# Six of eight output tiles of the mixer's first projection half as seven block products for eight

## The chip, the cores and the metric

The kernel runs on one core of one Trainium2 chip. The metric is device time in microseconds (us) of one execution. Engines are called as in the profile: PE (TensorE, the matmuls; PEld is its weight loading), DVE (VectorE), ACT (ScalarE), POOL (GpSimd) and SP (SyncE, which here only issues DMAs).

## The reference, cut to what matters

One layer of a hybrid decoder for 512 prompt tokens and 64 sample tokens, 576 in all, in float32:

```python
y_ssd = rms(y_ssd * silu(z)) * g_ssm_out                       # Mamba heads, 1024 wide
h_ml  = rms(h_ml) * g_mlstm_out * sigmoid(og)                  # mLSTM heads, 1024 wide
mix   = concatenate([y_ssd, h_ml], axis=-1) @ w_out            # 2048 -> 1024
x     = x + rms(mix) * g_post_mix
# then cross attention with w_xq, w_xo, and the gated FFN with w_gate, w_up, w_down
```

The change concerns `y_ssd @ w_out[:1024]`, the first half of the output projection.

## The kernel before, in words

Activations lie with features on the 128 partitions and the 576 tokens along the free axis, in 8 slices of 128 features. Every float32 operand of a matmul is split into a high part (a cast, by ACT) and a low part (source minus high, by DVE or, for half of some weight tiles, by a copy with scale -1 and an accumulating DMA that POOL issues). A product is then three matmuls: high by high, high weights by low activations, low weights by high activations. One output tile of 128 features over 8 slices is 24 matmuls for 256 tokens and 24 for 320 (`HALVES`).

The stretch around the change, in the order of the code:

- **The og tiles.** Eight tiles of the input projection (`in_tile(29 + j, og_evac(j))`), each in two token halves, gate the mLSTM output. A half's result lies in a PSUM bank of a pool of three (`GP`). DVE evicts it into a tile `tmp` (L1133; two buffers), ACT takes tanh, and DVE multiplies into `qk` (L1136). In the second half, POOL copies the 64 sample columns of `tmp` to `ogs` (L1138), and this `tmp` is free only then.
- **The mLSTM scan** of four heads runs beside it (L960 to L1005), as does the scan of the samples (L1029 to L1075). A head does four chunks one after another: matmuls `ps_n` (L983, L985) and `ps_c` (L988), a copy of `ps_n` by DVE (L986) and a state update `cst_` by DVE (L993, or L991 by ACT for the first). Then the head norm: squares by ACT (L938), short DVE steps (L941 to L954) around a power by POOL (L950), a scaling by DVE (L1000), eight transposes by PE (`ps_ht`, L1004). Each updated sample state leaves by a DMA of its tile (`o_cs`, L1059).
- **`mixs`**, the normed Mamba output `y`, is scaled (L1122) and split (L202, L203) in two groups of four slices, `gn_apply(0)` and `gn_apply(1)`.
- **`out1(j)`**, j from 0 to 7: the first half of the output projection, each with its weight tile split by ACT and DVE (L191, L198), the result copied to `f_mix` by ACT (L1154).
- **`out2(j)`**: the second half, from the mLSTM output `mixm`, added to `f_mix` by DVE (L1288). In the `out1` stretch the next stages are prepared: parts of later weights are split and stored (`presplit`), and the memory inputs are loaded (`memraw`).

No table sets the order here: the framework decides, when the program is built, the order of the instructions on each engine, by the times that it expects. On the chip each engine then goes through its list in that order. Where a pool's memory lay under another tile before, the first writer waits for what last used it.

The names that the prediction uses: "tile 2" and "tile 3" are the og tiles with j = 2 and j = 3, "head 3" is the last head of the scan.

Of the kernel before, what the change touches and what calls it, by code (L numbers as in the profile page):

```python
# [24 lines left out]
KT = 8  # L25
# [90 lines left out]
def build(nc, tc, ctx, I, O):  # L116
# [84 lines left out]
    def split(hi, lo, src, eng=None, cast=None):  # L201
        c = (cast or A.copy)(hi, src)  # L202
        (eng or V).tensor_tensor(lo, src, hi.bitcast(F32), op=ALU.subtract)  # L203
        return c
# [912 lines left out]
    def gn_apply(g):  # L1117
# [3 lines left out]
        for j in range(4 * g, 4 * g + 4):  # L1121
            V.scalar_tensor_tensor(y[:, j, :], y[:, j, :], PAR("g_ssm", j), rb, op0=ALU.mult, op1=ALU.mult)  # L1122
# [19 lines left out]
    for j in range(8):  # L1142
        in_tile(29 + j, og_evac(j))
        if j in GN:
            GN[j]()

    f = SL(5, "f_mix")
    evs = []

    def out1(j):  # L1150
# [6 lines left out]
    for j in range(8):  # L1157
        hm = qk[:, 4 * (j % 2) + j // 2, 0:TP]
        with tc.issue_after((evs[0] if j > 2 else htc).ins):
            A.activation(mixm_h[:, j, 0:TP], hm, AF.Copy, scale=ghalf[:, j:j + 1])  # L1160
        V.scalar_tensor_tensor(mixm_l[:, j, 0:TP], hm, ghalf[:, j:j + 1], mixm_h[:, j, 0:TP].bitcast(F32),
                               op0=ALU.mult, op1=ALU.subtract)
    o4 = ogs.rearrange("p (h d) t -> p h d t", d=2)
    for d in range(2):
        V.scalar_tensor_tensor(o4[:, :, d], o4[:, :, d], 1.0, qk[:, 4 * d:4 * d + 4, TP:T], op0=ALU.add, op1=ALU.mult)
    V.tensor_tensor(ogs, ogs, ghalf.unsqueeze(2).to_broadcast([P, KT, TS]), op=ALU.mult)
    split(mixm_h[:, :, TP:T], mixm_l[:, :, TP:T], ogs)
    stv.close()
# [61 lines left out]
    at = st.enter_context(tc.tile_pool(name="attn", bufs=1, reuse_waits="tile"))  # L1230


    PRE = [("xo", 0), ("xo", 1), ("g", 0), ("u", 0), ("g", 1), ("u", 1), ("g", 2), ("u", 2)]
    pre = dr.tile([P, len(PRE), 1024], F32, name="pre")

    ahead = []

    def presplit(n, left=1):

        while len(ahead) > left:  # L1240
            n_, t_ = ahead.pop(0)
            h_ = at.tile([P, 1024], F32R, name="preh", tag="prh", bufs=1)
            with tc.issue_after(evs[-1].ins):
                A.copy(h_, t_)
            V.tensor_tensor(t_, t_, h_.bitcast(F32), op=ALU.subtract)
            G.dma_start(pre[:, n_, :], t_)
        for _ in range(n):
            n_ = turns.pop(0)
            k, j = PRE[n_]
            t_ = at.tile([P, 1024], F32, name="prel", tag=("pr", "prl", "mv")[n_ % 3], bufs=1)  # L1250
            G.dma_start(t_, I[{"xo": "wxo", "g": "wgate", "u": "wup"}[k]][j])
            ahead.append((n_, t_))

    turns = list(range(len(PRE)))
# [7 lines left out]
    for j in range(8):  # L1262
        if j:
            out1(j)
        presplit(min(len(turns), 1 if j else 2))

        if j > 3:
            k2 = slice(2 * j - 8, 2 * j - 6)
            with tc.issue_after(loads[-1].ins):
                S.dma_start(memraw[:, k2, :], I["memT"][:, k2, :])  # L1270

    def memory(ks):
        for k in ks:
# [588 lines left out]
    class Seven:  # L1862
# [73 lines left out]
        def bank(s):  # L1936
            return (MP if s.side else GP)("ps_" + s.name)[:, :288]
# [539 lines left out]
```

## Time and profile before

| | us |
|---|---|
| median of three runs | 1074.99 (1074.83 to 1075.98) |
| the profiled execution, its time | 1074.69 |
| the profiled execution, its span | 1072.9 |
| from the first og eviction to the start of `out1` | 317.2 to 384.3 |
| `out1` | 384.3 to 434.2 |
| `out2` and what lies beside it | 434.2 to 488 |

The span is from the first to the last instruction; the execution's time is 1.8 us more. Durations of single matmuls in the profile overlap, since they are pipelined: what a stream of them costs is read from the distance of their starts. The lines themselves are shown in the prediction.

### The profile page before, as it was taken

Reading aid. Unit: us, or ns where it says so; the run is one execution under the profiler, and the core shown is the slowest. Engines: PE = TensorE matmul, PEld = TensorE weight load, DVE = VectorE, ACT = ScalarE, POOL = GpSimd, SP = SyncE. Lnnn points to the kernel's source line nnn. Section 1 sums busy time; section 2 is a strip of 40 time slices with the busy share of each in tenths; the row PEclk is TensorE's granted clock in tenths of the full one; section 3 lists DMA queues with packets and bytes.
Section 4 is the critical chain, followed back from the end, with each engine's and each line's share of the span. In section 5 each row is a group of like instructions: output and inputs, shape, how many; then the busy total and the mean of one; then the engine's idle time right before and its main releaser. Section 6 shows DMA issues by size and latency. Waiting matters only on the chain.

```text
span 1072.9 us, 20686 instructions
## 1 busy us (share of the span) xinstructions
PE 1063.1 (99%) x8096; PEld 1011.0 (94%) x8096; DVE 757.7 (71%) x1523; ACT 608.9 (57%) x1102; POOL 231.0 (22%) x305
## 2 busy tenths in 40 slices
PE   9999999999999999999999999999999999999997
PEld 8999887778999999999999989999999999999997
DVE  6798775658878774758755556766467887787556
ACT  7778523345654555655555445645566566656654
POOL 0454543313213111000154201100011111111000
PEclk9999999999999999999999999999999999999999
DMA  6776544425655349642468775743476687578532
GB/s 209 176 162 132 158 134 172 147 89 168 196 150 152 106 143 330 235 170 98 158 213 288 265 256 176 254 124 98 133 179 137 160 188 178 114 191 188 144 119 89
DMA packets 58965, 181.74 MB, mean 169 GB/s; under 512 B 6604, under 2 KB 12108, under 8 KB 58356
## 3 DMA queue, kind: packets, MB, share of 16 engines
q1 hardware_dynamic: 42884, 138.22, 38.7%
q0 software_dynamic: 15408, 41.43, 19.7%
q8 instruction: 63, 1.03, 0.4%
q10 hardware_dynamic: 576, 0.79, 0.2%
q14 instruction: 34, 0.28, 0.1%
HBM read 159.75 MB, written 20.65 MB: 168 GB/s over the span
## 4 chain that ended last, share of the span: by engine, by line
PE 98%; DVE 0%; DMA 0%; POOL 0%; issue 0%; ACT 0%; SPq 0%; DVEq 0%
PE ps_in L215 7%; PE ps_in L218 7%; PE ps_in L216 7%; PE ps_v L882 5%; PE ps_g L1946 3%; PE ps_u L1946 3%; PE ps_g L1945 3%; PE ps_o L218 3%; PE ps_o L216 3%; PE ps_u L1947 3%; PE ps_g L1947 3%; PE ps_o L215 3%; PE ps_u L1945 3%; PE ps_dn L1945 2%; PE ps_dn L1947 2%; PE ps_dn L1946 2%
## 5 line engine op out<-in xcount | busy, mean ns | idle before, releaser
L215 PE MATMUL ps_in<-uh,whi 128*128 128x320 f32 (+1 forms) x544 | 162.6, 299 | 0.0
L218 PE MATMUL ps_in<-uh,wlo 128*128 128x320 f32 (+1 forms) x544 | 161.6, 298 | 0.0
L216 PE MATMUL ps_in<-ul,whi 128*128 128x320 f32 (+1 forms) x544 | 161.1, 296 | 0.0
L191 ACT CAST whi<-raw 128x1024 fp32r<-128x1024 f32 (+1 forms) x104 | 105.4, 1015 | 93.3 <-PE ps_in L216 21.5
L198 DVE TENSOR_TENSOR wlo<-raw,whi 128x1024 fp32r<-128x1024 f32 (+2 forms) x97 | 95.3, 983 | 63.7 <-ACT whi L191 63.0
L215 PEld LDWEIGHTS ps_in<-uh,whi 128*128 128x128 f32 x544 | 102.3, 188 | 1.9 <-issue 0.8
L218 PEld LDWEIGHTS ps_in<-uh,wlo 128*128 128x128 f32 x544 | 102.2, 188 | 1.9 <-issue 1.3
L216 PEld LDWEIGHTS ps_in<-ul,whi 128*128 128x128 f32 x544 | 102.4, 188 | 0.5
L196 POOL DMA_DIRECT2D wlo<-win x31 | 27.2, 877 | 80.2 <-ACT wlo L195 69.9
L1945 PE MATMUL ps_g<-b,whi 128*128 128x288 f32 x144 | 42.4, 295 | 0.0
L1946 PE MATMUL ps_g<-b,whi 128*128 128x288 f32 x144 | 42.3, 294 | 0.0
L1946 PE MATMUL ps_u<-b,whi 128*128 128x288 f32 x144 | 42.2, 294 | 0.0
L1945 PE MATMUL ps_u<-b,whi 128*128 128x288 f32 x144 | 42.2, 294 | 0.0
L1905 DVE TENSOR_TENSOR wlo<-sw,whi 128x1024 fp32r<-128x1024 f32 (+1 forms) x26 | 29.6, 1139 | 16.8 <-ACT whi L1904 16.8
L1918 ACT CAST whi<-rawx 128x1024 fp32r<-128x1024 f32 (+1 forms) x26 | 25.6, 986 | 26.2 <-PE ps_dn L1946 13.3
L1895 ACT CAST whi<-raw 128x1024 fp32r<-128x1024 f32 (+1 forms) x26 | 25.6, 985 | 22.8 <-PE ps_g L1946 11.8
L215 PE MATMUL ps_xo<-qh,whi 128*128 128x288 f32 x128 | 38.2, 301 | 0.0
L216 PE MATMUL ps_xo<-ql,whi 128*128 128x288 f32 x128 | 37.8, 297 | 0.0
L218 PE MATMUL ps_o<-mixm_h,wlo 128*128 128x256 f32 (+1 forms) x128 | 37.5, 293 | 0.0
L216 PE MATMUL ps_o<-mixm_l,whi 128*128 128x256 f32 (+1 forms) x128 | 37.5, 293 | 0.0
L218 PE MATMUL ps_xq<-u2h,wlo 128*128 128x320 f32 (+1 forms) x128 | 37.5, 294 | 0.0
L218 PE MATMUL ps_o<-mixs_h,wlo 128*128 128x320 f32 (+1 forms) x128 | 37.4, 293 | 0.0
(788 smaller groups left out, 3855.6 us busy)
## 6 DMA issues: line engine op xcount, KB each, us to landing
raw<-win SPq DMA_DIRECT2D x35, 512.0 KB, 4.4
raw<-wout SPq DMA_DIRECT2D x17, 512.0 KB, 4.2
raw<-wxq SPq DMA_DIRECT2D x13, 512.0 KB, 4.7
raw<-wgate SPq DMA_DIRECT2D x13, 512.0 KB, 3.3
raw<-wup SPq DMA_DIRECT2D x13, 512.0 KB, 4.7
wlo<-win POOLq DMA_DIRECT2D x24, 256.0 KB, 5.6
kva<-vc SPq DMA_DIRECT2D x11, 512.0 KB, 5.9
raw<-wv SPq DMA_DIRECT2D x10, 512.0 KB, 4.0
```

What stands on the lines that cost most here:

```text
L191: casts.append(A.copy(hi[:, :n], raw[:, :n]))
L196: accs.append(G.dma_start(lo[:, a:b], src[:, a:b], accum_op=ALU.add))
L198: e.tensor_tensor(lo[:, a:b], raw[:, a:b], hi[:, a:b].bitcast(F32), op=ALU.subtract)
L215: mm(ps, wh, ah, start=i == 0, stop=False)
L216: products.append(mm(ps, wh, al, start=False, stop=False))
L218: m = mm(ps, tiles[order[c]][1], xh(order[c], t0, n), start=False, stop=c == len(tiles) - 1)
L882: mm(ps, a, b, skip_group_check=True, **kw)
L1895: s.c1 = A.copy(s.h1[:, s.all], s.r1[:, s.all])
L1905: V.tensor_tensor(s.l2[:, s.all], sw[:, s.all], s.h2[:, s.all].bitcast(F32), op=ALU.subtract)
L1945: mm(ps, wh, b[0][k], start=start and k == 0, stop=False, skip_group_check=True)
L1946: mm(ps, wh, b[1][k], start=False, stop=False, skip_group_check=True)
L1947: m = mm(ps, wl, b[0][k], start=False, stop=k == nk - 1, skip_group_check=True)
```

## The change

`out1` stays for output tiles 0 and 1. Tiles 2 to 7 are taken in three pairs (`Mixed`). In a pair the 1024 input features are two blocks of 512, the 576 tokens two blocks of 288 (`EHALVES`), the 256 outputs two blocks of 128. Seven products of sums of blocks then stand for eight; each has 4 slices by 3 matmuls of 288 columns, 84 matmuls for a pair where two `out1` had 96. The four sums of `y` blocks are made once by `mixed_sums` on DVE, in place, and split into `tmh` and `tml` (four tiles of 1152 columns each). The weight sums are made for each pair on DVE and split by ACT, DVE and accumulating DMAs. ACT copies a first result of an output block to `f_mix`, DVE adds the second.

What else moves: `mixm_parts` (the split of the mLSTM output) goes into the pairs, a third at a time, behind their last weight steps; three of the eight splits of later weights go into the pairs as a copy and an accumulating DMA (`low_ahead`), the other five into the `out2` loop; the `memraw` loads come behind the pairs. `ghalf` is written over its own parameter columns.

For room, the sums lie in a new pool on the right side of the memory (`mixsums`), and **`ogs`** moves into that pool from `zp`.

```diff
-    ghalf = ml.tile([P, KT], F32, name="ghalf")
-    V.tensor_scalar(ghalf, PAR("g_ml"), 0.5, None, op0=ALU.mult)
+    ghalf = PAR("g_ml")
+    V.tensor_scalar(ghalf, ghalf, 0.5, None, op0=ALU.mult)
...
+    sos = ExitStack()
+    wo = sos.enter_context(tc.tile_pool(name="mixsums", bufs=1, side="right", reuse_waits="tile"))
+    tmh, tml = [[wo.tile([P, 4, 288], F32R, name=k + str(m), tag=k + str(m)) for m in range(4)] for k in ("tmh", "tml")]
+    ES = [slice(t0, t0 + n) for t0, n in EHALVES]
+    (M11, M12), (M21, M22) = [[y[:, 4 * k:4 * k + 4, c] for c in ES] for k in range(2)]
...
+    def mixed_sums(*ops):
+        for m, o, p, q in ops:
+            V.tensor_tensor(o, p, q, op=ALU.subtract)
+            split(tmh[m], tml[m], o)
...
-    ogs = zp.tile([P, KT, TS], F32, name="ogs")
+    ogs = wo.tile([P, KT, TS], F32, name="ogs")
...
+    mixed_sums((0, M11, M12, M11), (2, M12, M22, M12), (1, M22, M22, M11), (3, M21, M21, M22))
...
+            for out, raw, w in ((l1, s.r1, src[0]), (l3[:, HA], s.r2[:, HB], src[1][:, HB])):
+                A.activation(out, raw, AF.Copy, scale=-1.0)
+                G.dma_start(out, w, accum_op=ALU.add)
+            A.copy(h1, s.r1)
+            V.tensor_tensor(sm[:, HB], s.r2[:, HA], s.r2[:, HB], op=ALU.add)
+            V.tensor_tensor(sm[:, HA], sm[:, HB], s.r1[:, HA], op=ALU.subtract)
+            split(h2, l2, sm)
+            V.tensor_tensor(s.r2[:, HA], s.r1[:, HA], s.r2[:, HA], op=ALU.subtract)
+            V.tensor_tensor(d4, s.r1[:, HB], sm[:, HA], op=ALU.subtract)
+            A.copy(h3, s.r2)
+            V.tensor_tensor(ls, k4(s.r2[:, HA]), k4(h3[:, HA]).bitcast(F32), op=ALU.subtract)
+            s.cast = A.copy(h4, k4(d4))
+            s.low = V.tensor_tensor(k4(l3[:, HB]), k4(d4), h4.bitcast(F32), op=ALU.subtract)
...
+        def mul(s, ps, w, b, start=True):
+            fh, fl = s.w[w]
+            for k in range(4):
+                mm(ps, fh[:, k, :], b[0][k], start=start and k == 0, stop=False, skip_group_check=True)
+                mm(ps, fh[:, k, :], b[1][k], start=False, stop=False, skip_group_check=True)
+                m = mm(ps, fl[:, k, :], b[0][k], start=False, stop=k == 3, skip_group_check=True)
+            return m
...
+        def early(s):
+            s.x, y_ = s.bank(), s.bank()
+            s.mul(s.x, 0, m11)
+            s.put(0, 0, s.x, True)
+            s.mul(y_, 1, m21)
+            s.put(0, 0, y_, False)
+
+        def mid(s):
+            s.mul(s.x, 2, tm[1], False)
+            s.put(0, 1, s.x, True)
+            s.z = s.bank()
+            s.mul(s.z, 3, tm[0])
+            s.mul(s.x, 4, tm[2], False)
+            s.put(1, 1, s.x, True)
+            s.put(1, 1, s.z, False)
+
+        def late(s):
+            s.mul(s.x, 5, tm[3], False)
+            s.put(1, 0, s.x, True)
+            s.mul(s.z, 6, m22, False)
+            s.put(0, 1, s.z, False)
...
     out1(0)
...
+    out1(1)
+    before = None
+    for j in (2, 4, 6):
+        pair_ = Mixed(j)
+        pair_.early()
+        if before:
+            before.late()
+        pair_.mid()
+        before = pair_
+        low_ahead()
+        mixm_parts(range(*{2: (0, 3), 4: (3, 6), 6: (6, 8)}[j]), pair_)
+        if j == 6:
+            with tc.issue_after(pair_.low.ins):
+                mixm_samples()
+    before.late()
```

The new pool changes the order around the og tiles, which the diff does not show. In the changed kernel L1148 is the copy to `ogs` (L1138 before), L1143 the eviction of an og half (L1133), L1127 the scaling of `y` (L1122); the scan's lines keep their numbers. Behind the brackets stand the queues and engines whose signals a row waits for; DMAHW are DMAs issued by SP, DMASW those issued by POOL.

POOL's list before, in the stretch of og tiles 0 to 2 (`rg0_y`, `rg1_y` are powers of the group norm, `hn_y_3032` is head 2's power):

```order
L1138 COPY ogs_4029<-tmp_4092 128x64 [waits Activation_49]
L196 DMA wlo_4291<-win 128x512 [waits DMASW7_49,Activation_49]
L273 TENSOR_TENSOR rg0_y_4107<-rg0_v_4106,c32_78 128x5 [waits DVE_49]
L1138 COPY ogs_4029<-tmp_4177 128x64 [waits Activation_49]
L196 DMA wlo_4358<-win 128x512 [waits DMASW0_49,Activation_49]
L273 TENSOR_TENSOR rg1_y_4192<-rg1_v_4191,c32_78 128x5 [waits DVE_49]
L950 TENSOR_TENSOR hn_y_3032<-hn_v_3031,c32_78 128x4 [waits DVE_49,Pool_49]
```

and now, with the copies of tiles 0, 1, 2 and 3 (`hn_y_3429` is the samples' power, `hn_y_3125` that of head 3):

```order
L950 TENSOR_TENSOR hn_y_3429<-hn_v_3428,c32_78 128x1 [waits DVE_49]
L950 TENSOR_TENSOR hn_y_3125<-hn_v_3124,c32_78 128x4 [waits DVE_49,Pool_49]
L1148 COPY ogs_4039<-tmp_4102 128x64 [waits DMAHW5_49,DMAHW7_49,DMAHW1_49,DMAHW0_49]
L1148 COPY ogs_4039<-tmp_4187 128x64
L1148 COPY ogs_4039<-tmp_4272 128x64 [waits Activation_49]
L1148 COPY ogs_4039<-tmp_4360 128x64 [waits Activation_49]
L196 DMA wlo_4523<-win 128x512 [waits DMASW2_49,Activation_49]
```

The first copy now waits for four DMAs of SP and stands behind the power of head 3, the last of the scan; before, tile 0's and tile 1's copies came ahead of head 2's.

DVE's list now, from the first of the four block sums (L1132) over the rest of head 3's norm to the evictions of tile 2 (`tmp_4243`, `tmp_4272`):

```order
L1132 TENSOR_TENSOR xs_94<-xs_94 128x4x288 [waits DVE_49]
L947 TENSOR_TENSOR hn_v_3124<-hn_d_3120 128x4 [waits DVE_49]
L948 TENSOR_TENSOR hn_v_3124<-hn_v_3124,hn_ss_3115 128x4 [waits DVE_49,Activation_49]
L949 TENSOR_SCALAR hn_v_3124<-hn_v_3124 128x4 [waits DVE_49]
L951 TENSOR_TENSOR hn_a_3126<-hn_y_3125 128x4 [waits Pool_49]
L952 SCALAR_TENSOR_TENSOR hn_a_3126<-hn_a_3126,hn_v_3124 128x4 [waits DVE_49]
L953 SCALAR_TENSOR_TENSOR hn_a_3126<-hn_a_3126,hn_y_3125 128x4 [waits DVE_49]
L954 TENSOR_TENSOR hn_a_3126<-hn_a_3126,hn_d_3120 128x4 [waits DVE_49]
L1000 TENSOR_SCALAR num_3082<-num_3082,hn_a_3126 128x256 [waits DVE_49]
L1000 TENSOR_SCALAR num_3082<-num_3082,hn_a_3126 128x256 x3
L1143 TENSOR_TENSOR tmp_4243<-ps_in_4218,rxb_95 128x256 [waits Pool_49]
L1143 TENSOR_TENSOR tmp_4272<-ps_in_4247,rxb_95 128x320 [waits Pool_49]
```

Both evictions of tile 2 stand behind the whole norm of head 3. Before, the first of them stood between two steps of head 2's norm (here `hn_d_3027`, `hn_v_3031`), with a wait for PE alone:

```order
L942 TENSOR_TENSOR hn_d_3027<-hn_d_3027,expnm_90 128x4 [waits DVE_49]
L1057 SCALAR_TENSOR_TENSOR c0_3372<-c0_3372,vt4_1796,ps_cu_3389 128x258 [waits PE_49]
L943 RECIPROCAL hn_d_3027<-hn_d_3027 128x4 [waits DVE_49]
L1133 TENSOR_TENSOR tmp_4233<-ps_in_4208,rxb_95 128x256 [waits PE_49]
L947 TENSOR_TENSOR hn_v_3031<-hn_d_3027 128x4 [waits DVE_49]
```

PE's list now, behind the 24 matmuls of tile 3's first half: part of head 3's scan (its eight transposes L1004, of which the first two are shown last, then tile 3's second half, `ps_in_4335`):

```order
L983 MATMUL ps_n_3083<-vt4_1795,dm_3063 128x257 [waits DVE_49]
L988 MATMUL ps_c_3086<-vt4_1795,kw_3080 128x257 [waits DVE_49]
L983 MATMUL ps_n_3090<-vt4_1795,dm_3063 128x257 [waits PE_49]
L988 MATMUL ps_c_3094<-vt4_1795,kw_3080 128x257 [waits DVE_49]
L985 MATMUL ps_n_3090<-cst__3088,qs_3060 128x257 [waits Activation_49,Pool_49]
L983 MATMUL ps_n_3098<-vt4_1795,dm_3063 128x257
L985 MATMUL ps_n_3098<-cst__3096,qs_3060 128x257 [waits DVE_49]
L988 MATMUL ps_c_3102<-vt4_1795,kw_3080 128x257
L983 MATMUL ps_n_3106<-vt4_1795,dm_3063 128x257 [waits DVE_49]
...
L1004 MATMUL ps_ht_3140<-c32_78,num_3082 128x128 [waits DVE_49]
L1004 MATMUL ps_ht_3146<-c32_78,num_3082 128x128
...
L215 MATMUL ps_in_4335<-uh_92,whi_4300 128x320 [waits DVE_49]
```

Before, these matmuls stood singly between those of tiles 4 and 5, and the transposes ahead of `out1`.

More of the change, by code (lines that the diff above doesn't have):

```diff
@@ L1145, in build, with mixm_parts @@
             GN[j]()
+    mixed_sums((0, M11, M12, M11), (2, M12, M22, M12), (1, M22, M22, M11), (3, M21, M21, M22))
+    def mixm_parts(js, p_):
+        for j in js:
+            hm = qk[:, 4 * (j % 2) + j // 2, 0:TP]
+            with tc.issue_after(p_.cast.ins):
+                A.activation(mixm_h[:, j, 0:TP], hm, AF.Copy, scale=ghalf[:, j:j + 1])
+            with tc.issue_after(p_.low.ins):
+                V.scalar_tensor_tensor(mixm_l[:, j, 0:TP], hm, ghalf[:, j:j + 1], mixm_h[:, j, 0:TP].bitcast(F32),
+                                       op0=ALU.mult, op1=ALU.subtract)
@@ new lines, in mixm_samples @@
+    def mixm_samples():
+        o4 = ogs.rearrange("p (h d) t -> p h d t", d=2)
+        for d in range(2):
+            V.scalar_tensor_tensor(o4[:, :, d], o4[:, :, d], 1.0, qk[:, 4 * d:4 * d + 4, TP:T], op0=ALU.add, op1=ALU.mult)
+        V.tensor_tensor(ogs, ogs, ghalf.unsqueeze(2).to_broadcast([P, KT, TS]), op=ALU.mult)
+        split(mixm_h[:, :, TP:T], mixm_l[:, :, TP:T], ogs)
+    stv.close()
+    svs = ExitStack()
+    wv = svs.enter_context(tc.tile_pool(name="mixweights", bufs=1, reuse_waits="tile"))
@@ new lines, in presplit @@
+    def presplit(n, left):
+        while len(ahead) > left:
+            n_, t_ = ahead.pop(0)
+            h_ = at.tile([P, 1024], F32R, name="preh", tag="prh", bufs=1)
+            with tc.issue_after(evs[-1].ins):
+                A.copy(h_, t_)
+            V.tensor_tensor(t_, t_, h_.bitcast(F32), op=ALU.subtract)
+            G.dma_start(pre[:, n_, :], t_)
+        for _ in range(n):
+            n_ = turns.pop(0)
+            t_ = at.tile([P, 1024], F32, name="prel", tag=("pr", "prl", "mv")[n_ % 3], bufs=1)
+            G.dma_start(t_, ahead_src(n_))
+            ahead.append((n_, t_))
@@ L1156, in build @@
     out1(0)
[L1157 to L1168, printed above, removed]
+    out1(1)
[13 more added lines that the diff above has]
+    before.late()
+    svs.close()
+    sos.close()
     phs = ExitStack()
@@ L1230, in build @@
     at = st.enter_context(tc.tile_pool(name="attn", bufs=1, reuse_waits="tile"))
[L1233 to L1254, printed above, removed]
     memh = at.tile([P, 2, KT, 256], F32R, name="memhl")
@@ L1261, in build @@
     ssqm, ssq = ssq_tile("ssqm"), ssq_tile("ssqo")
[L1262 to L1270, printed above, removed]
+    presplit(2, 0)
+    for j in range(4):
+        k2 = slice(2 * j, 2 * j + 2)
+        with tc.issue_after(loads[-1].ins):
+            S.dma_start(memraw[:, k2, :], I["memT"][:, k2, :])
     def memory(ks):
```

45 lines of the change are left out of this document (44 added, 1 removed).

## The prediction

> **What bounds the kernel now.** I read the busy shares first, then the chain of work that ended last, then the engines' busy time in the three stretches around the change.
>
> ```profile
> PE 1063.1 (99%) x8096; PEld 1011.0 (94%) x8096; DVE 757.7 (71%) x1523; ACT 608.9 (57%) x1102; POOL 231.0 (22%) x305
> PE 98%; DVE 0%; DMA 0%; POOL 0%; issue 0%; ACT 0%; SPq 0%; DVEq 0%
> 310.00:384.30 74.30, 74.30 (x566) 70.46 (x566) 57.80 (x158) 36.74 (x78) 17.60 (x23) 1.00 0.43 119
> 384.30:434.20 49.90, 49.90 (x387) 49.90 (x386) 29.80 (x40) 29.32 (x52) 6.91 (x13) 1.00 0.76 261
> 434.20:488.00 53.80, 53.80 (x419) 53.54 (x418) 35.20 (x61) 33.49 (x57) 3.84 (x7) 1.00 0.54 194
> ```
>
> The columns of the last three are the length, then busy time and instructions of PE, PEld, DVE, ACT and POOL, the granted clock, the DMA share and GB/s. PE is 98% of the chain and full in all three stretches, at clock 1.00. Two things follow. A matmul that goes is worth its whole time, wherever it stood. And any wait of PE that is new is paid in full, since there is no idle time to take it up. DVE has 57.8 of 74.3 us busy in the stretch with the scan and the og tiles; it is the second bound, and the one to watch.
>
> **What goes: 36 matmuls.** `out1` has 384 matmuls in 49.9 us, 0.130 each, the mean of 256 and 320 columns, so an output tile is 49.9/8 = 6.24 us. The pairs use 288 columns. Their pace is seen in the FFN, as the distance of starts:
>
> ```profile
> 899.77 0.29 PE L1945 MATMUL ps_u<-b,whi 128*128 128x288 f32 x1
> 899.90 0.29 PE L1946 MATMUL ps_u<-b,whi 128*128 128x288 f32 x1
> ```
>
> Also 0.13. Each pair has 84 for 96, three pairs 36 fewer: 36 x 0.130 = **-4.7 us**.
>
> **What moves: the evictions of tile 2.** `ogs` now lies where the samples' states lay, and its first copy waits for the DMAs that carry these states out. Before, the copies had no such wait.
>
> ```profile
> 323.53 0.62 POOL L1138 COPY ogs<-tmp 128x64 f32<-128x64 f32 x1 [6.22 <-ACT tmp L1134]
> 344.82 0.33 SPq L1059 DMA_DIRECT2D o_cs<-c  x1
> ```
>
> The first copy ran at 323.5; the last of these DMAs is issued at 344.8, so it couldn't have started before that. The copies are now listed behind head 3's power on POOL. With both `tmp` buffers held, tile 2's evictions stand on DVE behind all of head 3's norm, and PE's three banks fill up: tile 2's halves and tile 3's first. Tile 3's second half needs the bank of tile 2's first, so PE, in order, stops ahead of `ps_in_4335` until head 3 is through the scan, the norm and its scaling. What stands there now has these durations before:
>
> ```profile
> 341.37 0.16 DVE L954 TENSOR_TENSOR hn_a<-hn_a,hn_d 128x4 f32<-128x4 f32 x1
> 342.47 1.13 DVE L1000 TENSOR_SCALAR num<-num,hn_a 128x256 f32<-128x256 f32 x4
> 343.93 0.86 DVE L1057 SCALAR_TENSOR_TENSOR c<-c,vt,ps_cu 128x258 f32<-128x258 f32 x2
> 344.71 0.68 DVE L198 TENSOR_TENSOR wlo<-raw,whi 128x512 fp32r<-128x512 f32 x1
> 345.31 4.04 DVE L1122 SCALAR_TENSOR_TENSOR xs<-xs,par,ssqg 128x576 f32<-128x576 f32 x4
> 349.27 1.11 DVE L966 SCALAR_TENSOR_TENSOR dm<-ps_d,CT,c 128x128 f32<-128x128 f32 x4
> 351.08 0.69 DVE L973 TENSOR_TENSOR dm<-dm,ps_s 128x512 f32<-128x512 f32 x1
> 351.76 0.67 DVE L978 TENSOR_TENSOR kw<-ps_k,wendm 128x512 f32<-128x512 f32 x1
> ```
>
> Head 2's norm ends at 341.5 in both kernels. Behind it DVE's list has, in this order, 1.13 + 2 x 0.86 + 0.68 + 1.11 + 4.04 + 0.69 + 0.67 = 10.0 us and small steps, 0.4: `kw` is done at 351.9. Then the four chunks, each waiting for the one ahead:
>
> ```profile
> 355.72 0.36 ACT L991 COPY cst__3089<-ps_c 128x257 f32<-128x257 f32 x1
> 358.54 0.48 DVE L993 SCALAR_TENSOR_TENSOR cst__3097<-cst__3089,scalem,ps_c 128x257 f32<-128x257 f32 x1 [0.56 <-PE ps_c L988]
> 358.77 0.60 PE L985 MATMUL ps_n<-cst__3089,qs 128*128 128x257 f32 x2
> 359.20 0.60 PE L983 MATMUL ps_n<-vt,dm 128*128 128x257 f32 x2
> 359.40 0.43 DVE L986 COPY num<-ps_n 128x257 f32<-128x257 f32 x1 [0.39 <-PE ps_n L985]
> ```
>
> From the start of `ps_n` (358.77) to the end of its copy (359.83) is 1.06 us, and a state update costs about as much; one `ps_n` or `ps_c` takes PE 0.43 (358.77 to 359.20). The first chunk, with an ACT copy behind a square, takes 1.8; five or six links of 1.1 follow, some of them with the samples' norm between. I get 358.25 for the last copy.
>
> ```profile
> 368.64 2.76 DVE L203 TENSOR_TENSOR mixs_l<-xs,mixs_h 128x576 fp32r<-128x576 f32 x4
> 380.53 1.33 POOL L950 TENSOR_TENSOR hn_y<-hn_v,c 128x4 f32<-128x4 f32 x1
> 382.68 1.14 DVE L1000 TENSOR_SCALAR num<-num,hn_a 128x256 f32<-128x256 f32 x4
> 371.64 0.42 DVE L1133 TENSOR_TENSOR tmp<-ps_in,rxb 128x256 f32<-128x256 f32 x1
> ```
>
> The list goes on with four L203, 2.76, and the first block sum (1152 columns where an L203 has 576 in 0.69: 1.38, an estimate), small steps 1.3, the power 1.33, four steps of 0.2, four scalings 1.14 and the eviction 0.42: 358.25 + 2.76 + 1.38 + 1.3 + 1.33 + 0.8 + 1.14 + 0.42 = 367.4. So tile 3's second half begins near 367.5.
>
> ```profile
> 347.54 0.31 PE L215 MATMUL ps_in<-uh,whi 128*128 128x320 f32 x1
> 349.87 1.05 PE L971 MATMUL ps_s<-qk 128*128 128x128 f32 x8
> 351.12 0.39 PE L216 MATMUL ps_in<-ul,whi 128*128 128x320 f32 x1
> 383.14 1.17 PE L1004 MATMUL ps_ht<-c,num 128*128 128x128 f32 x8
> 384.07 0.36 PE L215 MATMUL ps_o<-mixs_h,whi 128*128 128x256 f32 x1
> ```
>
> Before it began at 347.54, so it is 20.0 later. Of that, PE fills a part with work that it does later in the kernel before: `ps_s` and `ps_k` 1.25 (349.87 to 351.12), eleven scan matmuls of 0.43, 4.7, the transposes 0.93 (383.14 to 384.07) and two for the samples at the same rate, 0.2: 7.1. PE is empty for 20.0 - 7.1 = **+12.9 us**. Ends: if the `y` scaling, the L203s and the sum (4.04 + 2.76 + 1.38) fell elsewhere, 4.7; if every link of the chunks lost another 0.3 us, 15.
>
> **The clock.** The longest part of that gap is from the last `ps_n` to the first transpose, some 8 us. What PE's clock does in idle time is seen at the ends of the trace:
>
> ```profile
> 1.06 4.23 PE L337 MATMUL ps_warm<-wz 128*128 128x256 bf16 x19 [1.06 <-DVE wz L334]
> 1065.52 0.42 PE L2309 MATMUL ps_ft<-c,sw 128*128 128x128 f32 x2
> 1069.00:1070.00 1.00, 0.00 (x0) 0.00 (x0) 0.41 (x1) 0.00 (x0) 0.00 (x0) 1.00 1.01 371
> 1071.00:1072.00 1.00, 0.00 (x0) 0.00 (x0) 0.00 (x0) 0.00 (x0) 0.00 (x0) 0.50 0.15 53
> ```
>
> PE's last matmul ends at 1065.9; the clock stands at 1.00 until 1070 and at 0.50 in 1071 to 1072. So a gap of 8 us halves it. At the start 19 matmuls of 256 columns take 4.2 us, 0.22 each, where half of `out1`'s pace would be about twice 0.115: half speed lasts up to 4 us of work. Of these 4 us, 1 lies beside the transposes, which wait for DVE anyway; 3 us at half speed lose **+1.5** (0 to 2).
>
> The Trainium skill, "TensorE: Matmul & The Clock Gate", section "Part 1: The HAM clock gate (the "warmup" mystery)", gives one window of about 3.4 us for both ways: idle that long, the clock halves, and as long a time of sustained work brings it back. By that rule the loss would be (3.4 - 1)/2 = 1.2, an estimate, and the sum 0.3 less. The trace of before agrees on the fall, which comes 4 to 5 us behind the last matmul.
>
> **DVE behind.** With head 3 done, DVE still owes the rest. Between the evictions of tile 4's second half and of tile 7's first it has five evictions 2.3, low weight parts, the second `y` scaling 4.04 and L203 2.76, three sums and three `tml` of 1.38, and five L1136:
>
> ```profile
> L198 DVE TENSOR_TENSOR wlo<-raw,whi 128x1024 fp32r<-128x1024 f32 x18 | 22.0, 1224 | 17.4 <-ACT whi L191 17.4
> L1136 DVE SCALAR_TENSOR_TENSOR qk<-tmp,qk 128x256 f32<-128x256 f32 x12 | 5.0, 424 | 0.6 <-ACT tmp L1134 0.5
> ```
>
> 2.3 + 0.68 + 2 x 1.22 + 4.04 + 2.76 + 6 x 1.38 + 5 x 0.42 = 22.6 us. PE has in that time three tiles of 6.24 and half an `out1`, 2.8, with a few small ones: 21.7. So **+0.9** (0 to 3).
>
> **ACT in the pairs.** The second pair's high cast (L1207) stands on ACT behind the first's last cast and three parts of `mixm`:
>
> ```profile
> 385.20 1.96 ACT L1160 ACTIVATE mixm_h<-qk,ghalf 128x512 fp32r<-128x512 f32 x3
> L191 ACT CAST whi<-raw 128x1024 fp32r<-128x1024 f32 (+1 forms) x104 | 105.4, 1015 | 93.3 <-PE ps_in L216 21.5
> ```
>
> That is 1.96, half a cast (512 columns), 0.5, and a whole one of 1.02: 3.5 us if all shows, nothing if PE, which has products of 12 x 0.13 = 1.56 us to fill in with, covers it. I take a third, **+1.2**. The weight sums on DVE and the accumulating DMAs lie beside this, where DVE was busy 29.8 of 49.9 us: nothing. The splits that move to `out2` find 18 us of DVE and 20 of ACT free there: nothing, up to 5 if the loads, issued later, come late.
>
> **Sum.** -4.7 + 12.9 + 1.5 + 0.9 + 1.2 = +11.8. The profiled execution took 1074.69 (its span 1072.9 and 1.8 around it), 0.3 under the median of 1074.99: 1074.69 + 11.8 = **1086.5**.
>
> **The rivals.**
> - *PE's wait is not there, and the kernel is faster.* If tile 3's second half takes a bank that is not held by tile 2's first half, or the scan spreads out, the products' gain stands. Then -4.7 + 0.9 + 1.2 = -2.6: 1072.1, and 1070 without the last two. It decides if the eviction ends before 347.5 + 7.1 + 4.7 = 359.3. For it speaks that PE's list has matmuls up to there; against it, that DVE's list alone is past 351.9 before the first chunk. 6%.
> - *Half the wait.* DVE's links overlap better than I add them, and the `y` scaling lies in gaps of the chunks: PE empty 6 us and no loss of clock: -4.7 + 6 + 0.9 + 1.2 = +3.4, 1078, from 1072.8 to 1081. 8%, of which 5% within 0.2%.
> - *More is late.* `memraw` comes behind the pairs on SP's list, and in `out2` DVE has L203 and memory steps that wait for it, ahead of the evictions of `ps_o`. Each late one holds PE: 5 to 10 us more, 1091 to 1098. Against it, ACT and DVE were a third idle there. 13%.
> - *No saving.* If the pairs ran at `out1`'s length, for example because each product waits for its weight sum, -4.7 goes: 1091.2. The 288-column rows speak against. 3%.
>
> **How the numbers follow.** The forecast's own range is 1081 to 1091, 70%: the sum with the ends of the wait (8 less is the half-wait case), the clock, DVE and ACT. For 8 in 10 I go to 1079 and 1093. A measurement of this kernel can tell about 0.2% from no change, 1072.8 to 1077.1 around the median. Faster 6% (the first rival), same 5%, slower 89%.
>
> **What would show it.** In the changed kernel's trace: a gap on PE between about 350 and 367, in pieces of about 1 us and one of 8, put down to DVE; tile 3's second half starting near 367; the granted clock under 1.00 behind it; POOL's first L1148 copy behind L950 of head 3; the pairs and `out1` together near 45 us. Wrong would be a PE without a gap there, tile 2's first eviction before 359, or a loss that lies in `out2`.

## The result and the profile after

The changed kernel takes 1093.92 us (median of six runs, 1093.46 to 1095.46), the kernel before 1075.26 in the same rounds (also six, of which one took 2218.64 and the others 1074.29 to 1075.98). The ratio is 1.0178, 95% interval 1.0165 to 1.0192: 1.8% slower, 18.7 us. The prediction had the direction, but 1086.5, and its ranges end at 1091 (seven in ten) and 1093 (eight in ten), 2.9 and 0.9 short of it. The profiled execution has a span of 1093.1, 20.2 more than before; the stretches below account for these 20.2.

From the page of the changed kernel, the engines' busy shares and the chain's shares, and from its list of PE's waits (what for, us in total, times, longest):

```profile
PE 1065.7 (97%) x8060; PEld 1012.1 (93%) x8060; DVE 772.8 (71%) x1552; ACT 620.3 (57%) x1118; POOL 242.5 (22%) x314
PE 91%; DMA 3%; DVE 2%; issue 2%; ACT 1%; POOL 0%; SPq 0%; DVEq 0%; POOLq 0%; ACTq 0%
PE ps_o L1226 <- ACT f_mix L1234: 8.9, 1, 8.9
PE ps_ht L1004 <- DVE num L1000: 7.6, 1, 7.6
PE ps_o L1226 <- ACT whi L1207: 0.6, 1, 0.6
```

PE has 36 matmuls fewer, as it should, but is busy 2.6 us longer, and the chain is PE for only 91%. Two new waits of 8 us or so stand out. To place them I cut both traces at three matmuls: the group norm's `ps_rb` ahead of head 3's scan, the first of `out1`, and the first of the next stage (`ps_mk`). The two rows of before that the prediction doesn't show, then the three of the changed kernel:

```profile
342.04 0.80 PE L287 MATMUL ps_rb<-c,rg_r 128*128 128x128 f32 x5
484.50 0.28 PE L215 MATMUL ps_mk<-memhl,wmh 128*128 128x256 f32 x1
```

```profile
342.33 0.49 PE L287 MATMUL ps_rb<-c,rg_r 128*128 128x128 f32 x3
395.48 0.28 PE L215 MATMUL ps_o<-mixs_h,whi 128*128 128x256 f32 x1
504.68 0.28 PE L215 MATMUL ps_mk<-memhl,wmh 128*128 128x256 f32 x1
```

With `out1`'s start before at 384.07, the stretch from `ps_rb` to `out1` (the scan and the og tiles) went from 42.0 to 53.2, **+11.1**; that from `out1` to `ps_mk` (first and second half of the projection) from 100.4 to 109.2, **+8.8**. All else is within 0.3. The first is the loss that was forecast. The second should have been a gain of 3.5.

**The first gap**, in the timeline (start, length, engine, line; what ended an idle time in brackets):

```profile
358.58 1.36 DVE L1132 TENSOR_TENSOR xs<-xs 128x1152 f32<-128x1152 f32 x1
360.63 1.01 POOL L950 TENSOR_TENSOR hn_y<-hn_v,c 128x4 f32<-128x4 f32 x1 [8.89 <-DVE hn_v L949]
361.61 0.41 POOL L1148 COPY ogs<-tmp 128x64 f32<-128x64 f32 x2
362.48 1.14 DVE L1000 TENSOR_SCALAR num<-num,hn_a 128x256 f32<-128x256 f32 x4
362.89 1.97 PE L1004 MATMUL ps_ht<-c,num 128*128 128x128 f32 x8 [7.62 <-DVE num L1000]
363.54 0.82 DVE L1143 TENSOR_TENSOR tmp<-ps_in,rxb 128x256 f32<-128x256 f32 x2
364.51 0.61 PE L215 MATMUL ps_in<-uh,whi 128*128 128x320 f32 x1
```

POOL's first copies run at 361.6, behind head 3's power; tile 2's evictions come at 363.5, behind head 3's whole norm; tile 3's second half starts at 364.5 (before: 347.54). The copies don't wait for the states' DMAs any more by then:

```profile
L1059 SPq DMA_DIRECT2D o_cs<-c x8: 332/344/344, 272.9 to 346.0; - x8
DMA to landing us min/median/max: 4.3/4.7/6.1
```

The last is issued at 346.0 and none took over 6.1 us to land, so all were there by 352.1. What holds the first copy to 361.6 is its place in POOL's list behind the power, that is, the order the framework chose.

**The second gap**, on ACT, POOL and PE:

```profile
434.75 0.39 ACT L1234 COPY f_mix<-ps_o 128x288 f32<-128x288 f32 x1
445.60 1.06 ACT L1272 ACTIVATE prem<-prem 128x1024 fp32r<-128x1024 f32 x1 [10.46 <-DMA prem<-wgate]
446.57 0.38 ACT L1234 COPY f_mix<-ps_o 128x288 f32<-128x288 f32 x1
```

```profile
421.00 0.56 POOL L1271 DMA_DIRECT2D prem<-wxo  x1 [3.51 <-DMA pre<-prem]
425.97 0.85 POOL L1273 DMA_DIRECT2D prem<-wxo  x1 [4.41 <-ACT f_mix L1234]
432.86 0.56 POOL L1274 DMA_DIRECT2D pre<-prem  x1 [4.29 <-DMA prem<-wxo]
440.08 0.55 POOL L1271 DMA_DIRECT2D prem<-wgate  x1 [6.66 <-DMA pre<-prem]
447.00 0.61 PE L1226 MATMUL ps_o<-tmh,whi 128*128 128x288 f32 x1 [8.94 <-ACT f_mix L1234]
```

This is `low_ahead`, the copy that takes a later weight's low part ahead: load (L1271), negative copy by ACT (L1272), the weight added by a DMA (L1273), store (L1274), all through one buffer. The second turn loads at 421.00 and frees the buffer at 440.08, 19.1 us later. Only then can the third load go out; ACT stands 10.46 us before its copy, with the copy to `f_mix` queued behind it that would free PE's bank. PE, which was done at 438.1, goes on at 447.0.

**The clock.** Behind each gap the granted clock (third last column) is low:

```profile
357.00:358.00 1.00, 0.00 (x0) 0.00 (x0) 1.00 (x4) 0.53 (x3) 0.00 (x0) 0.82 0.00 0
367.00:368.00 1.00, 1.00 (x5) 1.00 (x5) 1.00 (x1) 0.48 (x2) 0.46 (x1) 0.56 0.00 0
368.00:369.00 1.00, 1.00 (x9) 1.00 (x8) 1.00 (x4) 0.00 (x0) 0.29 (x1) 1.00 0.00 0
452.00:453.00 1.00, 1.00 (x6) 1.00 (x5) 0.00 (x0) 0.00 (x0) 0.55 (x2) 0.50 1.06 430
453.00:454.00 1.00, 1.00 (x8) 1.00 (x8) 0.00 (x0) 0.00 (x0) 0.70 (x4) 0.89 1.03 418
```

Cut at the edges of the half clock:

```profile
357.64:367.87 10.23, 4.98 (x21) 4.98 (x22) 6.28 (x18) 2.80 (x5) 1.73 (x4) 0.50 0.00 0
442.98:453.21 10.23, 6.21 (x24) 6.21 (x25) 1.68 (x2) 2.69 (x4) 1.65 (x5) 0.50 0.55 144
```

PE works at half clock from 362.9 to 367.9 and from 447.0 to 453.2: 5.0 and 6.2 us, of which half is lost, 2.5 and 3.1. Idle time and clock together are 10.4 of the first stretch's 11.1; the other 0.7 is not accounted for.

### The profile page after: what moved, and what is told of

It reads as the page before. It is cut to its first block, busy times and chain, and to the rows that moved or that the text cites. A ratio compares the mean times of both kernels' runs of the same rounds, so it can differ in the third digit from the quotient of the medians.

```text
span 1093.1 us, 20694 instructions
## 1 busy us (share of the span) xinstructions
PE 1065.7 (97%) x8060; PEld 1012.1 (93%) x8060; DVE 772.8 (71%) x1552; ACT 620.3 (57%) x1118; POOL 242.5 (22%) x314
## 4 chain that ended last, share of the span: by engine, by line
PE 91%; DMA 3%; DVE 2%; issue 2%; ACT 1%; POOL 0%; SPq 0%; DVEq 0%; POOLq 0%; ACTq 0%
PE ps_in L215 6%; PE ps_in L218 6%; PE ps_in L216 6%; PE ps_v L882 5%; PE ps_g L2064 3%; PE ps_u L2064 3%; PE ps_g L2063 3%; PE ps_u L2065 3%; PE ps_g L2065 3%; PE ps_u L2063 3%; PE ps_dn L2063 2%; PE ps_dn L2065 2%; PE ps_dn L2064 2%; PE ps_o L218 2%; PE ps_dn L215 2%; PE ps_dn L218 2%
## 5 line engine op out<-in xcount | busy, mean ns | idle before, releaser
L191 ACT CAST whi<-raw 128x1024 fp32r<-128x1024 f32 (+1 forms) x98 | 99.1, 1012 | 94.1 <-PE ps_in L216 19.3
L198 DVE TENSOR_TENSOR wlo<-raw,whi 128x512 fp32r<-128x512 f32 (+2 forms) x91 | 87.9, 967 | 66.0 <-ACT whi L191 64.9
L2013 ACT CAST whi<-raw 128x1024 fp32r<-128x1024 f32 (+1 forms) x26 | 25.6, 985 | 22.9 <-PE ps_g L2064 11.8
L215 PE MATMUL ps_o<-mixm_h,whi 128*128 128x256 f32 (+1 forms) x128 | 38.1, 298 | 0.0
L215 PE MATMUL ps_xq<-u2h,whi 128*128 128x320 f32 (+1 forms) x128 | 37.4, 295 | 0.0
```

The source lines that it names most:

```text
L191: casts.append(A.copy(hi[:, :n], raw[:, :n]))
L198: e.tensor_tensor(lo[:, a:b], raw[:, a:b], hi[:, a:b].bitcast(F32), op=ALU.subtract)
L215: mm(ps, wh, ah, start=i == 0, stop=False)
L2013: s.c1 = A.copy(s.h1[:, s.all], s.r1[:, s.all])
```

## The experiments

Each trace was cut at the same three matmuls. The times are medians, each ratio is to the kernel before in the same rounds, and the four stretches are those of the one execution that was profiled, which can be off the median (e8's took 1101.3, e15's 1098.0). The last column is from `ps_mk` to the end. e5, e6, e9, e10, e13 and e14 leave a part of the result out.

| kernel | time, us | ratio to before (95%) | to `ps_rb` | `ps_rb` to `out1` | `out1` to `ps_mk` | rest |
|---|---|---|---|---|---|---|
| before | 1075.3 | | 342.0 | 42.0 | 100.4 | 588.4 |
| changed | 1093.9 | 1.0165 to 1.0192 | 342.3 | 53.2 | 109.2 | 588.4 |
| e1 `ogs` elsewhere | 1096.4 | 1.0139 to 1.0209 | 342.0 | 45.2 | 119.0 | 588.9 |
| e2 two `low_ahead` | 1096.3 | 1.0177 to 1.0208 | 341.9 | 53.3 | 111.0 | 588.4 |
| e3 both | 1094.8 | 1.0166 to 1.0196 | 342.2 | 45.4 | 117.8 | 589.2 |
| e4 before, `ogs` moved | 1084.8 | 1.0068 to 1.0098 | 341.8 | 51.2 | 100.3 | 589.5 |
| e5 no splits | 1096.8 | 1.0184 to 1.0218 | 356.1 | 52.8 | 96.4 | 589.2 |
| e6 e1, no splits | 1092.2 | 1.0142 to 1.0172 | 357.4 | 45.2 | 98.8 | 588.9 |
| e7 e3, five splits | 1084.2 | 1.0065 to 1.0095 | 342.2 | 45.2 | 103.1 | 591.7 |
| e8 copy by POOL | 1097.1 | 1.0178 to 1.0230 | 344.0 | 52.9 | 113.8 | 588.8 |
| e9 as e5, held | 1097.5 | 1.0181 to 1.0213 | 357.6 | 53.0 | 96.4 | 588.9 |
| e10 e6, sums by POOL | 1094.9 | 1.0159 to 1.0192 | 356.1 | 47.0 | 101.3 | 588.4 |
| e11 store, then add | 1088.4 | 1.0084 to 1.0137 | 342.3 | 48.3 | 105.9 | 588.6 |
| e12 e11, six splits | 1092.0 | 1.0119 to 1.0172 | 343.2 | 48.3 | 109.3 | 590.4 |
| e13 splits gone | 1082.4 | 1.0046 to 1.0080 | 342.3 | 52.6 | 96.4 | 588.5 |
| e14 e1, splits gone | 1078.3 | 1.0013 to 1.0032 | 342.2 | 45.2 | 99.1 | 588.5 |
| e15 warm gap | 1094.2 | 1.0153 to 1.0199 | 342.1 | 51.1 | 114.8 | 588.4 |

### e4: the move of `ogs` alone

The kernel before, with

```diff
+    wo = sos.enter_context(tc.tile_pool(name="mixsums", bufs=1, side="right", reuse_waits="tile"))
+    wo.tile([P, 8, 4, 288], F32R, name="tms", tag="tms")
...
-    ogs = zp.tile([P, KT, TS], F32, name="ogs")
+    ogs = wo.tile([P, KT, TS], F32, name="ogs")
```

> The kernel before, with ogs alone moved to the right side, at the place that it has in the changed kernel (behind a tile of the size of the eight sums, which is not used). No products change. Theory: the first gap alone, a little shorter, since no block sum (1.4 us) stands within head 3's norm: 1075.3 + 10.4 - 1.4 = 1084.3. Rival (the wait comes from the block sums and their splits on DVE, not from where ogs lies): 1075 to 1077.

1084.76, and the longest wait of PE in the trace is the known one:

```profile
PE ps_ht L1004 <- DVE num L1000: 6.4, 1, 6.4
```

The theory holds: one tile of 2 KB per partition, moved to other memory with no product changed, costs 9.2 us in this stretch and nothing in the next (the rest of the kernel is 1.1 longer). It is the first gap.

### e1, e2, e3: each gap taken away

e1 writes the copies where they were before and moves them later:

```diff
+    ogz = zp.tile([P, KT, TS], F32, name="ogz")
...
-                G.tensor_copy(ogs[:, j, :], t[:, 256:320])
+                G.tensor_copy(ogz[:, j, :], t[:, 256:320])
...
+    G.tensor_copy(ogs, ogz)
```

> The changed kernel, but the eight copies go to a tile in zp, as before, and one POOL copy moves that tile to ogs after the last og tile. Theory (two separate waits of PE, the first from ogs' memory, the second from the third split of a later weight): the gap ahead of tile 3's second half goes with its slow clock, 7.9 us idle and 2.5 us of half speed; the second gap of 8.9 stays: 1093.9 - 10.4 = 1083.5, and the third POOL copy stands ahead of head 3's power. Rival (DVE has too much work in this stretch with the block sums, whatever the order): the wait moves behind the block sums, and less than 4 us come back: over 1089.

e2 has

```diff
-        low_ahead()
+        if j < 6:
+            low_ahead()
...
-    presplit(2, 0)
+    presplit(3, 0)
```

> The changed kernel, but the third pair makes no low_ahead; the out2 stretch begins with three instead of two of the later splits. Theory: ACT no longer waits 10.5 us for the third load in front of the copy to f_mix, so the second gap (8.9 us) goes with its 6.1 us of half clock (3.0 lost): 1093.9 - 11.9 = 1082.0. Rival (the second gap is the full DMA queues behind the pairs, 1.02 to 1.06 busy from 437 to 443, and any of the loads would hold PE): a weight of out2 is late instead, 3 us or less come back: over 1090.

e3 has both.

> Both edits, of e1 and of e2. Theory: only the products' saving and the small wait for the second pair's cast are left: 1075.3 - 4.7 + 0.6 = 1071.2, faster than both kernels. Rival (the pairs save less than 4.7, or DVE and ACT fall behind once the gaps no longer let them catch up): 1075 or more.

None of the three totals came: 1096.4, 1096.3, 1094.8. But the first stretch of e1 and e3 did, 45.2 and 45.4 for 53.2: 8.0 of the 11.1 us are gone, and lost again behind `out1`. In e1 the gap of 8.9 shrank to 1.2, and four waits further on, 10.0 us together, came in its place. In e3 the wait is now in `out2`; POOL, ACT, DVE and PE there:

```profile
479.97 0.54 POOL L1290 DMA_DIRECT2D prel<-wup  x1 [5.99 <-DMA pre<-prel]
489.57 1.05 ACT L1284 CAST preh<-prel 128x1024 fp32r<-128x1024 f32 x1 [8.83 <-DMA prel<-wup]
490.65 1.23 DVE L1285 TENSOR_TENSOR prel<-prel,preh 128x1024 f32<-128x1024 f32 x1 [8.79 <-ACT preh L1284]
491.79 0.48 DVE L1409 TENSOR_TENSOR f_mix<-f_mix,ps_o 128x320 f32<-128x320 f32 x1
492.33 0.58 PE L215 MATMUL ps_o<-mixm_h,whi 128*128 128x256 f32 x1 [5.91 <-DVE f_mix L1409]
```

The same pattern in another place: a load for a later split waits on POOL until an earlier store has landed, ACT's cast waits for the load, DVE's subtraction for the cast, and behind it on DVE stands the addition (L1409) that frees PE's bank. So the rivals of e1 and e2, "the wait moves", were nearer, though neither named this: the eight later splits act as one chain over both stages, and what is saved ahead of it or within it is waited out further on. From `ps_rb` to `ps_mk` the changed kernel takes 162.4 us, e2 and e1 164.2, e3 163.1.

### e8: the copy on another engine

```diff
-        A.activation(t_, t_.bitcast(F32), AF.Copy, scale=-1.0)
+        G.tensor_scalar(t_, t_.bitcast(F32), -1.0, None, op0=ALU.mult)
```

> The changed kernel, but POOL instead of ACT makes the negative copy in low_ahead, so ACT's copies to f_mix stand behind no load. Theory of the chain (the splits as a whole are too long for the pairs, and what is held only moves): PE waits in out2 instead, 1090 or more. Rival (one instruction in a bad place on ACT's list, nothing else): the second gap goes whole, 1082.

1097.1. ACT's copies no longer stand behind a load, and the second gap is gone from the pairs; PE then waits 3.6 and 7.2 us further on, at 472 and 493. The rival (one instruction in a bad place) falls. POOL's copy takes 2.9 us where ACT's took 1.06, which makes the chain a little longer still.

### e5, e9, e6: the later splits left out, with a flaw

The splits are replaced by one transfer each, `G.dma_start(pre[:, n_, :], ahead_src(n_))`; e9 puts it under an order of issue behind the first copy to `f_mix`, e6 adds e1's edit.

> The changed kernel with the splits of the eight later weights left out: each is one DMA from the weight to its place, no buffer, no work on ACT or DVE (this part of the result is not computed). Theory (the second loss is the chain of those splits: three transfers, one after another, on one buffer in the pairs, and what is moved out of the pairs comes late in out2): the first gap alone stays, 1075.0 + 10.5 - 4.7 + 0.6 = 1081.4. Rival (the loads for the memory, which come in one lump behind the pairs, or the weights behind them on SP's list hold PE): over 1087.

> e5 again, with the plain transfers of the later weights held back until the first copy to f_mix (in e5 they went out at the start of the program and delayed its first loads). The splits are left out. Theory: from the last step ahead of the scan to out1 11.1 us more than before, as in the changed kernel; from out1 to the first product of the next stage 4.0 less than before: 1075.2 + 11.1 - 4.0 = 1082.3. Rival (the gain of 4.0 seen in e5 came from transfers that were already done): 1087 or more.

> The copies elsewhere as in e1, and the later splits left out as in e5 (that part of the result is not computed). Theory: what e1 and e3 showed in out2 goes; the waits ahead of out1 and in the first pair stay (2.1 for the transposes, 1.4 for an og bank, 1.9 and 0.7 for weight sums, about 1 of half clock): 1075.0 - 4.7 + 7.1 = 1077.4. Rival (nothing hides the block sums on DVE once the first gap is away): over 1083. If the products' saving shows at all it shows here.

All totals missed (1096.8, 1097.5, 1092.2), because of the experiment: a transfer from memory to memory waits for nothing, so the framework issued all eight in the first 6 us, and in e9 too, where the order asked for did not hold them. They delay the program's first loads, and the column up to `ps_rb` is 14 to 16 us longer. The stage itself came as expected in e5 and e9: 96.4 twice, 4.0 less than before, with no wait of PE.

### e13, e14: the later splits left out for good

No splits and no transfers; the later stages read the weight itself in the low part's place:

```diff
     def low_ahead():
-        n_ = turns.pop(0)
...
+        turns.pop(0)
...
-            G.dma_start(lo, pre[:, low, :])
+            G.dma_start(lo, src)
```

> The changed kernel with the eight later splits left out altogether: no transfer into their place, and the later stages read the weight itself where they read the low part (so the result of these products is not the reference's; their times stay). Nothing is added at the start of the program, as it was in e5 and e9. Theory: the splits cost 12.8 us in the changed kernel; what stays is the first gap and the saving: 1075.5 + 11.1 - 4.0 = 1082.6. Rival (the time that e5 and e9 lost at the start was paid back by the shorter stage behind it, so the stage gains nothing by itself): 1088 or more.

1082.4, as the theory had it. `out1` to `ps_mk` is PE without a break; from e13 and from before, the stretch's length, busy times and clock:

```profile
394.86:491.25 96.39, 96.39 (x741) 96.37 (x740) 65.02 (x116) 61.58 (x107) 8.60 (x13) 1.00 0.61 186
```

```profile
384.07:484.50 100.43, 100.43 (x778) 100.41 (x778) 63.47 (x99) 60.95 (x105) 10.75 (x20) 1.00 0.65 228
```

So the products do save, 4.0 us. The splits in their new places cost 109.2 - 96.4 = **12.8**. The memory loads, one lump behind the pairs here as in the changed kernel, hold nothing. What in the splits costs the time is less sure: e13 takes away the chain and also its load on the DMA engines, whose share was 1.04 from 437 to 443.

> As e13, with the copies to ogs elsewhere as in e1. Theory: only the 3.2 us of DVE being behind ahead of out1, and e6's 1.6 gained behind it: 1075.5 + 3.2 - 1.6 = 1077.1, so the products' saving doesn't pay for the sums even with both losses away. Rival (the two losses were all): 1072 or less.

1078.3, 1.2 over the theory, and still slower than before. Its waits of PE that the kernel before doesn't have:

```profile
PE ps_ht L1004 <- DVE num L1000: 2.1, 1, 2.1
PE ps_o L1228 <- ACT whi L202: 1.5, 1, 1.5
PE ps_in L215 <- DVE tmp L1144: 1.4, 1, 1.4
```

The first and the third wait for DVE, where the awaited steps stand behind block sums. The second waits for ACT's cast of a weight sum, which stands behind a copy to `f_mix`. The three are 5.0 us, more than the 4.0 that the products save. So with both losses away the pairs' own cost on DVE and ACT takes the saving back: +3.2 ahead of `out1`, -1.3 behind it.

### e7, e11, e12, e10: shorter chains

e7 is e3 with five later weights in the list instead of eight; the other three are split where they are used.

> e3 (copies elsewhere, two low_ahead in the pairs) with five later weights split ahead instead of eight; the other three are split where they are used. Theory: out2 has three splits with a buffer each and no chain, so its waits (5.9, 1.0, 1.0 and the half clock, about 3) go: 1094.8 - 10.9 = 1083.9, if the stage that now splits three weights has room on ACT. Rival (the waits of out2 come from the memory loads): over 1091.

1084.2, as the theory had it: `out2` now has three splits with a buffer each. The stage that splits three weights itself pays 3.3 us.

e11 has e1's edit, two of the block sums by POOL, and in `low_ahead`

```diff
-        G.dma_start(t_, ahead_src(n_), accum_op=ALU.add)
-        G.dma_start(pre[:, n_, :], t_)
+        G.dma_start(pre[:, n_, :], t_.bitcast(F32))
+        G.dma_start(pre[:, n_, :], ahead_src(n_), accum_op=ALU.add)
```

> Copies elsewhere, two sums by POOL, and all eight later splits done, but in low_ahead the negative high part is stored first and the weight is added to it in its place, so that the buffer is held for two transfers instead of three. Theory (the length of the chain on one buffer decides): three times 13 us fit beside the pairs; of the 12.8 us that the splits cost in the changed kernel at most 5 are left: 1074.2 to 1079. Rival (the five splits in out2 are the hard part, whatever comes before): 1085 or more.

e12 adds a list of six weights, e10 has the sums by POOL without splits, with e9's flaw at the start.

> e11 with six later weights split ahead instead of eight, so that out2 has three, each with its own buffer and no reuse. Theory: no wait in out2, about 2 us more in the stage that now splits two weights itself (e7: 3.3 for three): 1076. Rival as for e11: 1082 or more.

> Copies elsewhere as in e1, the later splits left out and held back as in e9, and two of the four block sums of y by POOL instead of DVE. Theory (what is left ahead of out1, 3.2 us, is DVE being behind by the sums): 2 x 1.36 us less on DVE in front of head 3's norm, so the stretch up to out1 is 42.6 instead of 45.2, and with e6's 1.6 us less behind it the time is 1075.2 + 0.6 - 1.6 = 1074.2. Rival (POOL needs several us for a sum, and head 3's power waits behind it): the stretch is 45 or longer, 1077 or more.

The shorter hold of the buffer gives back some of what e1 lost behind `out1`, 105.9 for 119.0, but not the forecast 1074 to 1079. A turn of the buffer took 18.3 and 12.3 us in e11, for 24.7 and 21.5 in e1; the forecast had 13 each. The same bytes move, so this speaks for the hold of the buffer and not the load on the DMA engines, though the sums differ too. e11's rival has the right range but not the mechanism, since 5.0 of PE's 5.6 us of waits behind `out1` lie in the pairs. The sums by POOL were a mistake, as e10's rival had it (47.0 for the forecast 42.6): one takes POOL 2.6 us for DVE's 1.35, head 3's power stands behind it, and the wait for the transposes grows from 2.1 to 3.8 us.

e12 is slower than e11 where it should be faster, by 3.4 us in the stretch behind `out1`. Its waits of PE are 0.8 us longer in all; the rest is the clock. In both, PE waits 3.78 us for the transposes, at 385 to 389, and this is what follows, in e11 and in e12:

```profile
390.00:400.00 10.00, 10.00 (x73) 10.00 (x72) 8.47 (x11) 7.81 (x12) 2.73 (x3) 0.90 0.17 54
```

```profile
390.00:400.00 10.00, 10.00 (x59) 10.00 (x60) 8.28 (x13) 6.34 (x9) 2.09 (x2) 0.72 0.17 54
```

Over the five windows from 390 to 440 the clock's shortfall adds up to 2.7 us in e11 and 6.2 in e12, a part of it while PE waits. Why the clock differs so stays open. It is hardly the one profiled execution: the four of e11 lie between 1085.1 and 1090.4, those of e12 between 1090.1 and 1094.4.

### e15: the clock or the gap

70 matmuls of 208 columns between head 3's last `ps_n` and its transposes, with results that nothing reads:

```diff
+        if h == 3:
+            psw = MP("ps_w")
+            for _ in range(NDUM):
+                mm(psw[:, 0:208], c16[:, 0:128], c16[:, 0:208], start=True, stop=True, skip_group_check=True)
```

> The changed kernel with 70 matmuls of 208 columns, of no use, in the first gap, between head 3's last ps_n and its transposes (some 6.6 us of 7.6). Theory (2.5 of the 11.1 us are PE at half clock behind the gap): the stretch up to out1 is 50.6 instead of 53.15, the clock stays at 1.00 to 370, 1093.9 - 2.5 = 1091.4. Rival (what is slow behind the gap is not the clock but the weights or the moving data): 53.1, and 1093.9.

```profile
354.84 6.41 PE L1003 MATMUL ps_w<-c 128*128 128x208 bf16 x70
362.63 1.23 PE L1009 MATMUL ps_ht<-c,num 128*128 128x128 f32 x8 [1.39 <-DVE num L1005]
366.00:368.00 2.00, 2.00 (x17) 2.00 (x16) 2.00 (x4) 1.19 (x3) 0.75 (x1) 1.00 0.00 0
```

The clock stays at 1.00, and the stretch is 51.1 instead of 53.2: 2.1 of its 11.1 us were the clock (2.5 expected). The total doesn't tell: its median is 1094.2, of executions from 1092.1 to 1098.0, and the profiled one was the longest. In that one the chain behind took more than was gained, 114.8 us for 109.2.

No version here beats the kernel before. The best that computes everything is e7, 0.8% slower.

## Why the prediction was wrong

- **The saving** was right in kind and 0.7 too large: -4.7 forecast, -4.0 in e13, where PE has no gap from `out1` to `ps_mk`. A matmul of 288 columns took 0.132 us there from start to start, not 0.130; over the 252 that are left that is 0.6. The prediction's sign for it, `out1` and the pairs near 45 us, failed in the changed kernel: 62.7, with 27 matmuls of `out2` among them.
- **The first gap** was right in every link (copies behind head 3's power, tile 2's evictions behind its norm, PE stopped ahead of `ps_in_4335`) and too long in size. Forecast: tile 3's second half at 367.5, 12.9 us empty, of which some 8 from the last `ps_n` to the first transpose. Measured: 364.5, and 7.9 empty (7.62 and 0.24). So the 8 was right, and the chunks were the term: PE was to stand empty for the other 5 us between their links, and hardly did. `kw` was done at 350.2 (351.9 forecast) and the last copy at 355.7 (358.25). The 358.25 is also less than the links add up to, 351.9 + 1.8 + five or six times 1.1 = 359.2 to 360.3. The power took 1.01, not 1.33.
- **The clock**: 1.5 forecast for this gap; 2.5 by the half-clock stretch, 2.1 by e15. The Trainium skill, "TensorE: Matmul & The Clock Gate", section "Part 1: The HAM clock gate (the "warmup" mystery)", has the clock return after at least one busy window of about 3.4 us, and puts the scatter, which comes from where in the free-running window the work begins, at half a microsecond. Here it took 5.0 and 6.2 us, so the scatter is larger than the page's; the measurement decides. The lengths at half clock, 10.24 us both times, are three windows of 3.41, as the page's window would have it.
- **DVE behind**: 0.9 forecast, nothing seen in the changed kernel, since the long gap let DVE catch up. Without the gap (e14) the stretch is 3.2 longer than before, for waits behind the block sums: the term was real, and hidden by the loss it was added to. Here the two did not add.
- **ACT in the pairs**: 1.2 forecast, 0.6 measured (the wait for L1207), and in e13, without the splits, nothing.
- **The step that failed**: "The splits that move to `out2` find 18 us of DVE and 20 of ACT free there: nothing, up to 5 if the loads, issued later, come late." The three that stay in the pairs as `low_ahead` got no term at all. I priced the later splits by the engines' free time. What the runs showed is the time of transfers, one after another, on one buffer. The row for it was in the trace of before, the landing time of the loads of the same splits (L1251), minimum, median and maximum:

```profile
DMA to landing us min/median/max: 4.7/7.8/10.2
```

  Three such transfers, a cast and the issues are 17 us at the least and some 26 at the median, an estimate; three turns, 50 to 78, do not fit beside 45 us of `out1` and pairs. Measured: 21.3 and 19.1 for a turn, and 12.8 us lost, of which 8.9 are the second gap, 3.1 its clock and 0.6 the wait for L1207.
- **The rivals**: the time lies in the band of "more is late" (1091 to 1098, 13%), but not by its mechanism. That was the memory loads; e13 keeps them and has no wait in the stage.
- **Luck**: two errors of opposite sign made the forecast look closer than it was. The first stretch was forecast at +15.3 (12.9 + 1.5 + 0.9) and came at +11.1, the second at -3.5 (-4.7 + 1.2) and came at +8.8. With the first one right, the forecast would have been 4 us further off.

## What to carry to other kernels

Price what an edit moves, not only what it adds: a transfer that held no one before needs its landing times added up along its buffer, and compared with the length of the stage that it moves to. Where engines work in order, one instruction that waits for such a transfer holds whatever is queued behind it, and mending that place moves the wait to the next. A tile moved to other memory inherits the waits of what lay there, and the order that is built around them can cost more than the waits: ask for its last reader, DMAs among them, before its size.

## What was not expected of the hardware

- After a gap PE's clock stayed at half for 5.0 and 6.2 us of work (5.0 behind 7.6 us without matmuls, 6.2 behind 8.9). The fall came 2.4 us behind the last matmul in one case (355.3 to 357.6) and 4.9 in the other (438.1 to 443.0).
- The clock's answer to a gap isn't fixed by its length: the same wait of 3.78 us was followed by ten us at a mean clock of 0.90 in one trace and 0.72 in another (e11, e12). What these traces show is that half clock comes in lengths of one, two or three times 3.41 us, the program's end apart. It lasted 3.41 behind that wait in e11 (388.67 to 392.08), 6.83 in e12 (388.77 to 395.60), 10.24 twice in the changed kernel, whose two falls lie 85.3 us apart, 25 times 3.41. A gap of 2.13 us ahead of `ps_ht` was enough for 3.41 us of half clock in e3 (387.13 to 390.54) and cost no clock in e1. So where a gap falls in a grid of 3.41 us seems to decide; no run here moves a gap in this grid on purpose.
- Eight transfers of 0.5 MB from memory to memory, issued in the first 6 us, cost the program's start 14 us (e5: `ps_rb` at 356.1 for 342.0), though nothing waits for them.
- Half a megabyte landed between 3.5 and 9.0 us after its issue in the changed kernel's splits (`low_ahead`).
